# A tenth column block of the expert keys on TensorE, and eight expert blocks with a raw float32 high part

## Chip, core and metric

One core of one Trainium2 chip runs the whole program. The metric is device time in microseconds (us), the median of three runs of the kernel: 2496.15 before, from 2490.72 to 2497.42. Engines are named as in the profile: PE is the matrix engine (PEld its weight loads), DVE the vector engine, ACT the scalar engine, POOL the general one, SP issues DMA.

## What is computed

One step of a hybrid decoder layer: an input projection, an RWKV-7 group and a sparse-attention group, an output projection, a layer norm, and a PEER mixer (128 x 128 experts, of which each token picks 16 in each of 8 heads), followed by a second layer norm. There are 256 prompt tokens and 32 sample tokens, with 2048 columns. Only the mixer matters here:

```python
def block(args):
    xb, eb, gb = args
    h = jax.nn.gelu(jnp.einsum('cd,chkd->chk', xb, u_tab[eb]), approximate=False)
    return jnp.einsum('chk,chkd->cd', gb * h, v_tab[eb])
```

`u_tab` and `v_tab` have 16384 rows of 2048 float32, `eb` holds the 128 chosen experts of each token, and `gb` their gates.

## The kernel before, in words

The program is written in Python against a tile framework. A scheduler simulates the engines and puts the instructions of each engine in an order; each engine then runs its own queue strictly in that order. `tc.high_priority` lets a group go ahead, `tc.issue_after(x)` holds a group back until instruction x is placed.

The product of a token with its 128 chosen rows of `u_tab` is split by columns. UG of the 2048 columns (896 before) are done on DVE: POOL issues a gather of one chosen row per token (`fetch`, 128 tokens at a time, tile `rows`, five buffers), and one DVE instruction multiplies it with the tokens and sums it up (`dot`, line 1803). There are 256 such gathers and dots, 128 for each of two tiles of 128 prompt tokens. The other NDB blocks of 128 columns (9 before) are done on PE for all 16384 experts and all 256 prompt tokens, in 128 blocks of 128 experts (`dense`, lines 1873 to 1888): SP loads the transposed rows of the block (`ur`, three buffers), PE accumulates in one of five banks `ph`, ACT copies the result to the table AW. Six of the column blocks are split columns: ACT rounds the rows to float32r as high part `uh` (line 1639), DVE forms the low part `ul` (line 1640), in two halves of three column blocks each, and PE does three float32r matmuls for each column block, with XHd and XLd the high and low part of the tokens (line 1886). The rest of the column blocks (three before, tile Xfd) are multiplied as raw float32, straight from `ur` (line 1879).

The stages around it: the query stage ("wq") has PE do the queries and DVE choose the experts, head by head (lines 1364 to 1421, with POOL helping), and DVE do the sample tokens' dots (`sr`, line 1559). At its end come the exponential of the gates (`ge`, ACT, line 1428) and the Gelu of the sample tokens (`shT`, ACT, line 1565), which the scheduler mixes with the first blocks of the dense stage. AW lies where buffers of the query stage were, so that its first copy waits for them. Low and high parts of the first NPRI = 12 blocks have a high priority. In the dense stage one or two dots are issued behind each block's low parts: ND = 1, and one more in NDN of 8 blocks (4 before). What is left of the 256 is done in the weighing ("weigh"), spread over the first 28 of its 68 steps: a step makes one-hot tiles on DVE (`oo`, line 1918), transposes and multiplies them on PE, and DVE picks out the sums (`xj`, line 1941); in every other step DVE adds up eight sums (line 1944), ACT takes their Gelu (line 1945), and DVE multiplies with the result (line 1949) after the next `oo`. The last stage (V) multiplies the weights with `v_tab`.

Of the kernel before, what the change touches and what calls it, by code (L numbers as in the profile page):

```python
# [2 lines left out]

# [1 line left out]

# [5 lines left out]
F32 = mybir.dt.float32  # L11
F32R = mybir.dt.float32r
# [6 lines left out]
P = 128  # L19
# [3 lines left out]
NPR = 256  # L23
# [26 lines left out]
NDW = 1  # L50
NPRI = 12
ND = 1
NDN = 4
NUR = 3
NRW = 5
NDB = 9
SPLIT = ((0, 3), (3, 6))
NSP = SPLIT[-1][1]
UG = 128 * (16 - NDB)
# [93 lines left out]
def hybrid_decode_step(ctx: ExitStack, tc: tile.TileContext, a, outs, dbg=None):  # L153
    nc = tc.nc
    ve, sc, pe, gp, sy = nc.vector, nc.scalar, nc.tensor, nc.gpsimd, nc.sync
    stop = dbg.get("stop", 99) if dbg is not None else 99
# [1622 lines left out]
    dp, kc, kq = (Pool(nm, "left") for nm in ("dp", "kc", "kq"))  # L1779
    dp([P, NDB, P], "ur", bufs=NUR)  # L1780
    XHd, XLd = dp([P, NSP, NPR], "XHd", F32R), dp([P, NSP, NPR], "XLd", F32R)
# [42 lines left out]
    for h in range(9):  # L1824
        S = []
        for c in (2 * h, 2 * h + 1):
            if c < 16:
                pb = bank("pj")
                for o in range(0, 16, 8):
                    w = wq_.pop((c, o), None) or query_load(c, o)  # L1830
# [42 lines left out]
    def dense(i1):  # L1873

        w = dp([P, NDB, P], "ur", bufs=NUR)
        sy.dma_start(w.rearrange("p k e -> p (k e)"), a["peer_u_t"][P * i1:P * i1 + P, :])
        ph = bank("ph")
        for e in range(NSP, NDB):
            pe.matmul(ph[:, :NPR], w[:, e, :], Xfd[:, e - NSP, :], start=(e == NSP), stop=False)  # L1879
        for e0, e1 in SPLIT:  # L1880
            wh, wl = (dp([P, e1 - e0, P], nm, F32R, bufs=3) for nm in ("uh", "ul"))
            with tc.high_priority(offset=120 + 45 * i1 if i1 < NPRI else 0):
                lo_ = columns(w[:, e0:e1, :], wh, wl)
            for e in range(e0, e1):
                for wi, xi in ((wh, XHd), (wh, XLd), (wl, XHd)):
                    mm = pe.matmul(ph[:, :NPR], wi[:, e - e0, :], xi[:, e, :],  # L1886
                                   start=False, stop=(e == NSP - 1 and wi is wl))
        return lo_, mm, sc.copy(AW[:, i1 // 64, :, i1 % 64], ph[:, :NPR])  # L1888

    tabled = []  # L1890
    for i1 in range(P):
        lo_, mm, end = dense(i1)
        n_ = ND + (i1 * NDN % 8 < NDN)
        with tc.issue_after(lo_.ins):
            dot(min(max(P - got[1], 0) or n_, n_))
        if got[1] >= P + 8 and not tabled:
            with tc.issue_after(mm.ins), tc.issue_after(end.ins):
                table(0)
            tabled.append(0)
# [168 lines left out]
    for k in range(P):  # L2068
# [9 lines left out]
        lo_ = ve.tensor_tensor(vl, v_, vh.bitcast(F32), OP.subtract)  # L2078
# [92 lines left out]
```

## Time and profile before

| what | us |
|---|---|
| median of the runs | 2496.15 |
| the profiled execution, its own time | 2498.71 |
| its span, first to last instruction | 2496.9 |
| dense stage in the span | 1190.0 to 1682.3 |
| weighing, steps with dots | 1682.3 to 1818.2 |
| DVE busy in the span, line 1803 (the dots) | 272.0 |
| PE busy in the span, lines 1879 and 1886 (the dense stage) | 867.0 |

A busy time is a sum over the instructions of a group; what matters is whether the engine is the last to be ready in the stage where it works. PE's matmuls overlap each other in the table (a float32r matmul of 256 columns is shown with some 283 ns and follows the one before after 120), so that distances between starts are read instead. A row of the timeline has the start, the length, the engine, the line and the operation, out<-in with the tile names, and in brackets the idle time before it and what ended that.

### The profile page before, as it was taken

How to read it: one execution, taken by the hardware profiler on the slowest of the kernel's cores; microseconds unless marked ns; L12 is line 12 of the kernel's file. 1: busy time of each engine (PE TensorE's matmuls, PEld its weight loads, DVE VectorE, ACT ScalarE, POOL GpSimd, SP SyncE). 2: the span in 40 equal slices, each digit the busy share in tenths (PEclk: the TensorE clock that was granted, in tenths of full speed). 3: DMA queues.
4: the chain of work that ended last, by engine and by line, in shares of the span. 5: the costliest groups of instructions: out<-in, count | busy, mean ns of one | idle time of the engine just before them, and what ended most of it. 6: DMA issues, size and time to landing. Idle time of an engine off the chain costs nothing.

```text
span 2496.9 us, 44823 instructions
## 1 busy us (share of the span) xinstructions
PE 2246.1 (90%) x16396; PEld 1888.6 (76%) x16396; DVE 1851.9 (74%) x4241; ACT 927.4 (37%) x1848; POOL 1373.4 (55%) x1422
## 2 busy tenths in 40 slices
PE   7979999988889997789699999996699799999996
PEld 7967898875545665678598889986676688888785
DVE  5789756554563446889977776779976799988888
ACT  4433222213441333220233343434566444443433
POOL 5677423242444005478655555556656488876662
PEclk9999999998896896899899999997899899999998
DMA  7777975457668884797499999996678599999995
GB/s 219 234 235 232 272 220 172 122 178 223 214 206 269 283 299 148 282 325 241 144 385 372 370 361 357 353 336 221 216 249 294 221 369 356 362 365 361 350 358 186
DMA packets 327613, 684.23 MB, mean 274 GB/s; under 512 B 82270, under 2 KB 200992, under 8 KB 326464
## 3 DMA queue, kind: packets, MB, share of 16 engines
q1 hardware_dynamic: 246176, 342.58, 41.4%
q0 software_dynamic: 81216, 338.78, 38.4%
q8 instruction: 129, 2.11, 0.3%
q14 instruction: 92, 0.75, 0.1%
HBM read 665.69 MB, written 23.88 MB: 276 GB/s over the span
## 4 chain that ended last, share of the span: by engine, by line
PE 60%; DVE 17%; DMA 8%; issue 7%; ACT 4%; POOL 3%; SPq 1%; DVEq 0%; POOLq 0%; ACTq 0%
PE pb L2085 17%; PE ph L1886 10%; PE pj L426 8%; PE ph L1879 3%; PE pa L1668 3%; PE p L1083 2%; DVE rows L1803 2%; DMA co<-in_cache_cmp_kv,gidx 2%; DVE sr L1559 2%; PE pa L1963 2%; DVE ul L1640 2%; PE ss L1500 1%; PE px L1930 1%; PE fs L1982 1%; DVE oo L1918 1%
## 5 line engine op out<-in xcount | busy, mean ns | idle before, releaser
L457 POOL DMA_INDIRECT rows<-in_peer_u_g,gi x256 | 332.3, 1298 | 239.5 <-DVE rows L1803 195.2
L457 POOL DMA_INDIRECT rq<-in_peer_v_g,gi x256 | 378.6, 1479 | 141.8 <-DVE fP L2058 80.2
L1803 DVE SCALAR_TENSOR_TENSOR rows<-rows,x1a 128x896 f32<-128x896 f32 x256 | 272.0, 1092 | 2.9 <-DMA rows<-in_peer_u_g,gi 2.7
L1886 PE MATMUL ph<-XHd,ul 128*128 128x256 f32 x768 | 225.3, 294 | 27.6 <-DVE ul L1640 22.7
L426 PE MATMUL pj<-XH,wl 128*128 128x288 f32 (+1 forms) x752 | 230.1, 306 | 15.2 <-DVE wl L421 9.1
L426 PE MATMUL pj<-XH,wh 128*128 128x288 f32 (+1 forms) x752 | 228.2, 304 | 13.6 <-DVE ss L756 6.9
L1886 PE MATMUL ph<-XHd,uh 128*128 128x256 f32 x768 | 236.7, 308 | 0.0
L2058 DVE SCALAR_TENSOR_TENSOR fP<-rq,ge,fP 128x640 f32<-128x640 f32 x254 | 223.8, 881 | 5.9 <-DMA rq<-in_peer_v_g,gi 3.4
L426 PE MATMUL pj<-XL,wh 128*128 128x288 f32 (+1 forms) x752 | 224.5, 299 | 0.0
L1640 DVE TENSOR_TENSOR ul<-ur,uh 128x384 fp32r<-128x384 f32 x256 | 131.8, 553 | 120.1 <-ACT uh L1639 93.3
L1886 PE MATMUL ph<-XLd,uh 128*128 128x256 f32 x768 | 217.4, 283 | 0.0
L2085 PE MATMUL pb<-vl,ah 128*128 128x512 f32 (+1 forms) x768 | 207.8, 378 | 1.4 <-issue 0.5
L2085 PE MATMUL pb<-vh,ah 128*128 128x512 f32 (+1 forms) x768 | 188.0, 380 | 20.9 <-ACT vh L2077 20.9
L2085 PE MATMUL pb<-vh,al 128*128 128x512 f32 (+1 forms) x768 | 205.7, 376 | 0.0
L419 ACT CAST wh<-wraw 128x512 fp32r<-128x512 f32 (+1 forms) x188 | 114.7, 617 | 223.7 <-PE pj L426 169.0
L1879 PE MATMUL ph<-Xfd,ur 128*128 128x256 f32 x768 | 187.6, 380 | 1.1 <-DMA ur<-in_peer_u_t 1.1
L1886 PEld LDWEIGHTS ph<-XHd,ul 128*128 128x128 f32 x768 | 147.0, 192 | 42.1 <-DVE ul L1640 41.8
L2085 PEld LDWEIGHTS pb<-vh,ah 128*128 128x128 f32 x768 | 145.5, 196 | 43.8 <-ACT vh L2077 24.5
L480 DVE SCALAR_TENSOR_TENSOR CA<-co,wbc,CA 128x256 f32<-128x256 f32 x248 | 133.9, 577 | 45.5 <-DMA co<-in_cache_cmp_kv,gidx 45.2
L2085 PEld LDWEIGHTS pb<-vl,ah 128*128 128x128 f32 x768 | 145.2, 195 | 24.5 <-DVE vl L2078 4.5
L426 PEld LDWEIGHTS pj<-XH,wl 128*128 128x128 f32 (+1 forms) x752 | 142.6, 190 | 26.6 <-DVE wl L421 12.7
L1888 ACT COPY AW<-ph 128x256 f32<-128x256 f32 x128 | 77.8, 608 | 228.1 <-PE ph L1886 198.7
(854 smaller groups left out, 5472.6 us busy)
## 6 DMA issues: line engine op xcount, KB each, us to landing
ur<-in_peer_u_t SPq DMA_DIRECT2D x128, 576.0 KB
wraw<-in_w_in SPq DMA_DIRECT2D x152, 256.0 KB
cw<-in_w_out SPq DMA_DIRECT2D x32, 512.0 KB
wraw<-in_w_out SPq DMA_DIRECT2D x32, 512.0 KB
wraw<-in_peer_wq SPq DMA_DIRECT2D x32, 512.0 KB
cw<-in_peer_wq SPq DMA_DIRECT2D x32, 512.0 KB
wraw<-in_w_in SPq DMA_DIRECT2D x64, 128.0 KB
co<-in_state_win_kv SPq DMA_DIRECT2D x16, 512.0 KB
```

The costliest lines, as they stand in the source:

```text
L419: sc.copy(wh[:, :, :n], w[:, :, :n])
L426: last[2] = pe.matmul(pb[:n, :nt], wi[:, k, :n], xi[(o + k) // 8][:, (o + k) % 8, :nt], start=(o + k == 0 and wi is wh and xi is xh), stop ...
L457: gp.indirect_dma_start(out=dst, out_offset=None, in_=rows_, in_offset=bass.IndirectOffsetOnAxis(ap=ix, axis=0))
L480: ve.scalar_tensor_tensor(d_, x_, w_, d_, op0=OP.mult, op1=OP.add)
L1640: return ve.tensor_tensor(xl, pb, xh.bitcast(F32), OP.subtract)
L1668: pe.matmul(acc[t], xi[:, e, P * t:P * t + P], wi[:, e, :], start=(k == e == n_ == 0), stop=(k == 6 and e == 1 and n_ == 2))
L1803: i_ = ve.scalar_tensor_tensor(r_, r_, 1.0, X1a[t], op0=OP.mult, op1=OP.mult, accum_out=h_)
L1879: pe.matmul(ph[:, :NPR], w[:, e, :], Xfd[:, e - NSP, :], start=(e == NSP), stop=False)
L1886: mm = pe.matmul(ph[:, :NPR], wi[:, e - e0, :], xi[:, e, :], start=False, stop=(e == NSP - 1 and wi is wl))
L1888: return lo_, mm, sc.copy(AW[:, i1 // 64, :, i1 % 64], ph[:, :NPR])
L2058: ve.scalar_tensor_tensor(fP[t], r_, w_, fP[t], op0=OP.mult, op1=OP.add)
L2085: pe.matmul(acc[3 * t + q][:, :n_], wi[:, P * t:P * t + P], xi[:, 512 * q:512 * q + n_], start=(k == 0 and wi is ah and xi is vh), stop=(k ...
```

## The change

Ten column blocks go to PE and 768 columns stay with DVE (UG follows from NDB); the tenth is a raw one, four in place of three. NDN is 6, so that three in four dense blocks have two dots: 224 dots in the stage in place of 192, and 30 in place of 62 in the weighing (two are done before). In the first eight dense blocks (NFB) the six split columns are multiplied raw, `ur` with XHd, and only the product with XLd is a float32r one, with `uh`; no `ul` is formed, `uh` has no raised priority, and the dots of these blocks are not held back by their low parts. `uh` has two buffers in place of three. Lines after the edits are 1 to 10 higher.

```diff
-NDN = 4
+NDN = 6
...
-NDB = 9
+NDB = 10
+NFB = 8
...
         ph = bank("ph")
         for e in range(NSP, NDB):
             pe.matmul(ph[:, :NPR], w[:, e, :], Xfd[:, e - NSP, :], start=(e == NSP), stop=False)
+        if i1 < NFB:
+            for e in range(NSP):
+                pe.matmul(ph[:, :NPR], w[:, e, :], XHd[:, e, :].bitcast(F32), start=False, stop=False)
         for e0, e1 in SPLIT:
-            wh, wl = (dp([P, e1 - e0, P], nm, F32R, bufs=3) for nm in ("uh", "ul"))
+            if i1 < NFB:
+                wh = dp([P, e1 - e0, P], "uh", F32R, bufs=2)
+                lo_ = sc.copy(wh, w[:, e0:e1, :])
+                for e in range(e0, e1):
+                    mm = pe.matmul(ph[:, :NPR], wh[:, e - e0, :], XLd[:, e, :], start=False, stop=(e == NSP - 1))
+                continue
+            wh, wl = (dp([P, e1 - e0, P], nm, F32R, bufs=n_) for nm, n_ in (("uh", 2), ("ul", 3)))
...
-        with tc.issue_after(lo_.ins):
+        with tc.issue_after(lo_.ins) if i1 >= NFB else nullcontext():
             dot(min(max(P - got[1], 0) or n_, n_))
```

ACT's queue at the start of the dense stage, before; each `ur` number is one dense block, from block 1's second half on, and each `ph` number a block's bank:

```order
L1639 CAST uh_13421<-ur_13402 128x384
L1639 CAST uh_13444<-ur_13438 128x384
L1888 COPY AW_13356<-ph_13359 128x256
L1639 CAST uh_13457<-ur_13438 128x384
L1639 CAST uh_13483<-ur_13477 128x384
L1888 COPY AW_13356<-ph_13404 128x256
L1639 CAST uh_13496<-ur_13477 128x384
L1639 CAST uh_13519<-ur_13513 128x384
L1888 COPY AW_13356<-ph_13440 128x256
L1639 CAST uh_13532<-ur_13513 128x384
L1428 ACTIVATE ge0_73<-ge0_73 128x128
```

The same place after, where `ur_13393` is block 1, `ur_13420` block 2, `ur_13450` block 3 and `ur_13480` block 4:

```order
L1887 CAST uh_13406<-ur_13393 128x384
L1898 COPY AW_13356<-ph_13359 128x256
L1887 CAST uh_13411<-ur_13393 128x384
L1887 CAST uh_13433<-ur_13420 128x384
L1898 COPY AW_13356<-ph_13395 128x256
L1887 CAST uh_13438<-ur_13420 128x384
L1429 ACTIVATE ge0_73<-ge0_73 128x128
L1429 ACTIVATE ge1_74<-ge1_74 128x128
L1887 CAST uh_13463<-ur_13450 128x384
L1898 COPY AW_13356<-ph_13422 128x256
L1887 CAST uh_13468<-ur_13450 128x384
L1566 ACT_TABLE_LOAD
```

Block 1's second high part has moved behind the first AW copy, block 3's behind the gates' exponentials, and block 4's, with the Gelu of `shT` after the last row, behind that. Before, all of these stood ahead.

ACT in the middle of the dense stage, before, from the AW copy of one block on, and after:

```order
L1888 COPY AW_13356<-ph_15579 128x256
L1639 CAST uh_15619<-ur_15613 128x384
L1639 CAST uh_15632<-ur_15613 128x384
L1639 CAST uh_15658<-ur_15652 128x384
L1639 CAST uh_15671<-ur_15652 128x384
L1888 COPY AW_13356<-ph_15615 128x256
L1888 COPY AW_13356<-ph_15654 128x256
L1639 CAST uh_15694<-ur_15688 128x384
```

```order
L1898 COPY AW_13356<-ph_15600 128x256
L1640 CAST uh_15685<-ur_15678 128x384
L1640 CAST uh_15698<-ur_15678 128x384
L1898 COPY AW_13356<-ph_15640 128x256
L1640 CAST uh_15722<-ur_15715 128x384
L1640 CAST uh_15735<-ur_15715 128x384
L1898 COPY AW_13356<-ph_15680 128x256
```

Before, every second or third block's high parts stood behind the AW copy of the block just ahead of it (`ur_15688` behind `ph_15654`); after, both high parts of a block stand ahead of that copy throughout (`ur_15715` ahead of `ph_15680`).

DVE where the first low parts meet the dots, before, with the Gelu's input (`shT`):

```order
L1803 SCALAR_TENSOR_TENSOR rows,hd_12150<-rows,x1a 128x896
L1640 TENSOR_TENSOR ul<-ur,uh 128x384
L1564 TENSOR_TENSOR shT<-shT 128x32
L1430 RECIPROCAL sm_13341<-sm_13341 128x8
L1640 TENSOR_TENSOR ul<-ur,uh 128x384 x2
```

And after, where the input of the Gelu stands nine rows ahead of the first of these:

```order
L1804 SCALAR_TENSOR_TENSOR rows,hd_12150<-rows,x1a 128x768
L1432 TENSOR_TENSOR ge_74<-ge_74,sm_13347 128x128
L1815 TENSOR_SCALAR ii<-gi_70 128x128
L1804 SCALAR_TENSOR_TENSOR rows,hd_12150<-rows,x1a 128x768
L1816 CAST ii<-ii 128x128
L1804 SCALAR_TENSOR_TENSOR rows,hd_12150<-rows,x1a 128x768 x12
L1641 TENSOR_TENSOR ul<-ur,uh 128x384 x2
L1804 SCALAR_TENSOR_TENSOR rows,hd_12150<-rows,x1a 128x768 x2
```

Before, low parts ran between the last selections and the dots; after, 14 dots stand between the Gelu's input and the first low part, which is block 8's.

More of the change, by code (lines that the diff above doesn't have):

```diff
@@ L1 @@
 import math
-from contextlib import ExitStack
+from contextlib import ExitStack, nullcontext
 import numpy as np
```

## Prediction

> **What bounds the kernel now.** First the busy time by stage, in stretches cut where the trace changes character. The columns are the stretch, its length, busy us of PE, PEld, DVE, ACT and POOL (instructions in brackets), granted PE clock, DMA share and GB/s.
>
> ```profile
> core 0: us, PE busy (x) PEld busy (x) DVE busy (x) ACT busy (x) POOL busy (x), PEclk, DMA share, GB/s
> 1109.00:1190.00 81.00, 79.22 (x389) 70.06 (x388) 81.00 (x315) 7.80 (x22) 64.42 (x93) 1.00 0.80 243
> 1190.00:1221.40 31.40, 9.29 (x58) 8.14 (x56) 31.40 (x143) 2.48 (x6) 18.25 (x39) 0.71 0.22 72
> 1221.40:1226.50 5.10, 5.10 (x24) 5.04 (x24) 5.10 (x28) 1.54 (x4) 2.33 (x7) 0.50 0.86 285
> 1226.50:1682.30 455.80, 449.13 (x3000) 410.75 (x2999) 332.54 (x678) 179.92 (x378) 261.29 (x211) 1.00 0.96 356
> 1682.30:1818.20 135.90, 92.06 (x540) 84.62 (x539) 130.67 (x408) 62.34 (x168) 83.85 (x63) 0.77 0.70 219
> 1818.20:1967.00 148.80, 135.70 (x1026) 99.62 (x1025) 97.36 (x395) 94.34 (x250) 71.13 (x63) 0.96 0.69 230
> ```
>
> The dense stage is the third to fifth line with the second: it runs from 1190.0 to 1682.3. From 1226.5 on PE has no rest and the full clock. The sixth line is the first 28 steps of the weighing, which carry the dot products left over: there DVE is full and PE waits at a clock of 0.77. From 1190 to 1221.4 it is DVE too: PE has work for 9 us only. In the query stage (first line) both are full: the dense stage cannot start before 1190.0, and what is taken from DVE there brings all its later work forward. The change buys time of DVE and pays in time of PE, so it costs in one stretch and gains in another, and the sum is a difference of the two.
>
> Next the price of a block on PE, from its timeline. Each matmul is shown as longer than the distance to the next, so distances count.
>
> ```profile
> 1450.25 1.46 PE L1879 MATMUL ph<-Xfd,ur 128*128 128x256 f32 x6
> 1451.36 0.47 PE L1886 MATMUL ph<-XHd,uh 128*128 128x256 f32 x1
> 1451.66 0.28 PE L1886 MATMUL ph<-XLd,uh 128*128 128x256 f32 x1
> ...
> 1453.70 1.46 PE L1879 MATMUL ph<-Xfd,ur 128*128 128x256 f32 x6
> ...
> 1455.11 0.28 PE L1886 MATMUL ph<-XLd,uh 128*128 128x256 f32 x1
> 1455.46 0.38 PE L1886 MATMUL ph<-XHd,ul 128*128 128x256 f32 x1
> ...
> 1457.47 0.81 PE L1879 MATMUL ph<-Xfd,ur 128*128 128x256 f32 x3
> ```
>
> A block takes three raw float32 matmuls (six passes) and 18 float32r ones. From 1451.66 to 1453.70 there are 17 float32r matmuls: 0.120 us each. The block takes 3.45 us from 1450.25, so the six raw passes are left with 3.45 - 2.16 = 1.29, 0.215 each. The query stage says the same of raw passes alone:
>
> ```profile
> 1181.93 7.07 PE L1832 MATMUL pj<-XT,wraw 128*128 128x256 f32 x32
> 1188.84 1.34 PE L1378 MATMUL pb<-SKT,QP 128*128 128x128 f32 x8
> ```
>
> 32 passes in 6.91 us, 0.216 each: a raw matmul costs 0.432, a float32r one 0.120. The next block in the timeline takes 3.77, because PE stands from 1455.11 to 1455.46 for the low part. Over the long stretch 124 blocks take 455.8 us, 3.68 each, so 0.23 a block is this wait.
>
> Last, the start of the dense stage, on PE, ACT and DVE:
>
> ```profile
> 1190.01 1.46 PE L1879 MATMUL ph<-Xfd,ur 128*128 128x256 f32 x6
> 1221.40 0.58 PE L1886 MATMUL ph<-XHd,ul 128*128 128x256 f32 x1 [21.74 <-DVE ul L1640]
> ```
> ```profile
> 1205.70 0.59 ACT L1888 COPY AW<-ph 128x256 f32<-128x256 f32 x1 [10.90 <-issue]
> 1229.58 0.51 ACT L1428 ACTIVATE ge<-ge 128x128 f32<-128x128 f32 x2
> 1237.60 0.23 ACT L1565 ACTIVATE shT<-shT 128x32 f32<-128x32 f32 x1 [1.61 <-DVE shT L1564]
> ```
> ```profile
> 1117.72 0.54 DVE L1640 TENSOR_TENSOR ul<-ur,uh 128x384 fp32r<-128x384 f32 x1
> 1204.25 1.22 DVE L1559 SCALAR_TENSOR_TENSOR sr<-sr,sx 128x1024 f32<-128x1024 f32 x1
> 1220.80 0.55 DVE L1640 TENSOR_TENSOR ul<-ur,uh 128x384 fp32r<-128x384 f32 x1
> 1221.27 1.08 DVE L1803 SCALAR_TENSOR_TENSOR rows<-rows,x1a 128x896 f32<-128x896 f32 x1
> 1222.28 0.55 DVE L1640 TENSOR_TENSOR ul<-ur,uh 128x384 fp32r<-128x384 f32 x1
> 1236.91 0.55 DVE L1640 TENSOR_TENSOR ul<-ur,uh 128x384 fp32r<-128x384 f32 x1
> 1237.39 0.18 DVE L1564 TENSOR_TENSOR shT<-shT 128x32 f32<-128x32 f32 x1
> ```
>
> PE's gap of 21.7 us waits for a low part that DVE has no time for. The three rows of ACT are not about blocks: the first AW copy follows the last sample dot (DVE, 1204.25), the gates' exponential and the Gelu follow DVE's last selection of experts. All three stand in ACT's queue among the high parts.
>
> **The dense stage from the ninth block.** Each of the 120 blocks gets one raw matmul more: 2.16 + 4 x 0.432 = 3.89 us. Does the wait of 0.23 stay? In the changed order of ACT both high parts of the next block stand ahead of the AW copy, and the second can start as soon as the block ends. It then needs 0.51 (ACT) and 0.47 (DVE), and PE first asks for it after 1.73 + 1.08 + 0.24 = 3.05 us. DVE has 0.94 of low parts and 1.75 dots in a block. A dot costs 1.01 (1221.27 to 1222.28), and with 768 instead of 896 columns 0.88 by my estimate (0.87 in proportion, and some of it is fixed). That is 2.5 of 3.89 us. So I take 0.01 a block; bounds 0 and 0.1 (12 us).
>
> The DMA moves more: 590 to 655 KB of transposed rows a block, while the gathered rows stay at 688 KB (1.5 x 459, now 1.75 x 393). That is 1.28 MB in 3.68 us before (348 GB/s of the 356 shown) and 1.34 MB in 3.90 after, 345: no more than it gives now, but at a share of 0.96 there is no reserve, and part of the 0.1 is for that.
>
> In one place the Trainium skill would price this otherwise. FP8 and Floating Point Precision, TensorE Precision Notes, says that true FP32 takes four passes through the array. If a pass is the 0.120 of a float32r matmul, an estimate by that page is 0.48 a raw matmul and 4.08 a block, 23 us more in the stage. The trace has 0.432 in two stages, so the sum goes by that.
>
> **The first eight blocks.** Each takes ten raw matmuls and six float32r ones, 4.32 + 0.72 = 5.04 us, against 3.45: dearer on PE by 1.6, free of DVE. Low parts of these blocks were on DVE three times before 1190 and eight times from 1205 to 1237 (first and last of each are in the rows), 0.47 each, so the last sample dot ends 1.4 us sooner, the gates 4.4 sooner with the shorter dot, and the Gelu 5.4 sooner. ACT is still served in order. Block 0: 1190.0 to 1195.0. Block 1 does its raw matmuls by 1199.4, and its second high part stands behind the AW copy (1204.3) and is ready at 1205.4: end 1205.8. Block 2: 1210.9. Block 3 has its raw part by 1215.2, then waits for a high part behind the gates: 1225.2 + 0.51 + 0.51, one AW copy, the other half: end 1227.8. Block 4's raw part ends at 1232.1, its high part waits for the Gelu (1232.3): end 1234.5. Blocks 5 to 7: 1249.6. Bounds of 3 us either way.
>
> Block 8 needs its first low part 1.73 + 0.24 after that, at 1251.6. On DVE, 14 dots stand ahead of it behind the Gelu's input (rows of the order above), and these wait for gathers:
>
> ```profile
> 1237.19 1.16 POOL L457 DMA_INDIRECT rows<-in_peer_u_g,gi  x1
> ```
> ```profile
> 1242.06 1.09 DVE L1803 SCALAR_TENSOR_TENSOR rows<-rows,x1a 128x896 f32<-128x896 f32 x1
> 1244.71 1.09 DVE L1803 SCALAR_TENSOR_TENSOR rows<-rows,x1a 128x896 f32<-128x896 f32 x1 [0.41 <-DMA rows<-in_peer_u_g,gi]
> 1250.91 1.09 DVE L1803 SCALAR_TENSOR_TENSOR rows<-rows,x1a 128x896 f32<-128x896 f32 x1 [0.49 <-DMA rows<-in_peer_u_g,gi]
> ```
>
> The third gather is issued at 1237.19, behind DVE's selection, so now at 1232.4. From there DMA must bring 14 x 393 KB and four loads of 655 KB, 8.1 MB: 22.8 us at 356 GB/s. The last dot is done at about 1257 and the low part at 1257.5, so PE stands for 6 us. The bounds are 0 (DVE work alone: 14 x 0.88 and 3 us of small ones end by 1247.4) and 13 (dots 2.07 us apart, as from 1244.71 to 1250.91). After it PE is cold: in the stretch 1221.4 to 1226.5 above, 24 matmuls took 0.21 us each at a clock of 0.50. That is 2 us more. The Trainium skill (TensorE: Matmul & The Clock Gate, What's actually happening) has the half clock after one idle window of about 3.4 us; the trace agrees, 0.50 here.
>
> The dense stage ends at 1249.6 + 8 + 120 x 3.90 = 1725.6, which is 43 us later.
>
> **The weighing.** 62 dots were left for it, 30 now are (28 steps, one each, two steps with two).
>
> ```profile
> L1803 DVE SCALAR_TENSOR_TENSOR rows<-rows,x1a 128x896 f32<-128x896 f32 x62 | 65.0, 1086 | 1.1 <-DMA rows<-in_peer_u_g,gi 1.1
> L1918 DVE TENSOR_TENSOR oo<-CT,TB 128x1024 f32<-128x1024 f32 x30 | 36.6, 1220 | 0.0
> L1941 DVE SCALAR_TENSOR_TENSOR xj<-px,oo 128x128 f32<-128x128 f32 x112 | 32.4, 289 | 2.9
> ```
> ```profile
> 1749.17 1.22 DVE L1918 TENSOR_TENSOR oo<-CT,TB 128x1024 f32<-128x1024 f32 x1
> ...
> 1751.63 0.17 DVE L1944 TENSOR_TENSOR E<-E,TB 128x8 f32<-128x8 f32 x1
> 1751.72 1.08 DVE L1803 SCALAR_TENSOR_TENSOR rows<-rows,x1a 128x896 f32<-128x896 f32 x1
> ...
> 1753.76 0.20 ACT L1945 ACTIVATE E<-E 128x8 f32<-128x8 f32 x1
> ...
> 1754.75 1.22 DVE L1918 TENSOR_TENSOR oo<-CT,TB 128x1024 f32<-128x1024 f32 x1
> ```
>
> A step without dots is 2.55 us of DVE (1749.17 to 1751.72), 28 of them 71.4; with 62 x 1.01 that is 134, nearly the whole stretch. With 30 x 0.88 it is 97.8. What is late next is the Gelu: it ends at 1753.96, 2.24 after the sum that it reads, and DVE multiplies with its result behind the next one-hot tile. With two dots and that tile (1.14) DVE comes to it after 3.2; with one dot after 2.0, so it waits 0.3 in every other step, and where PE's clock is down, and with it what stands ahead of the Gelu on ACT, up to three times that by my estimate. 14 such waits are 4 to 13 us; I take 8. The stretch takes 106 instead of 136: 30 us gained, bounds 22 and 37. Later steps have no dots and stay.
>
> **Sum.** +43 - 30 = +13 us. The profiled execution took 2498.71 us, 1.8 more than its span, so it would take 2511.7. It lies 2.6 over the median of the runs, 2496.15, and the change of that median is the forecast: 2509 us.
>
> **Rivals.**
> *Break even.* The stall at block 8 does not come, since DMA moves more than 356 GB/s while PE asks for little, and the Gelu is in time: 1249.6 + 466.5 = 1716.1, +34, against -37. That is 2493. For it: DMA was nearly idle before 1221. Against it: the dots waited for gathers around 1250 even before.
> *Faster.* ACT does not hold the first eight blocks up: they run through in 40.3 us, to 1230.3, and 120 x 3.89 later it is 1697, +15, against -30: 2481. It decides at block 3: its last pass would have to be over by 1216. For it: PE is free and the loads are early. Against it: the order has the exponential ahead of that block's high part, and DVE reaches its input only at 1225.
> *Much slower.* DMA, at a share of 0.96, becomes the bound, or the loop of high part, low part and copy costs 0.2 a block again: 24 us more, 2533. A weighing held by PE at half clock adds up to 8 to either.
> *Not as described.* The raw blocks could be built otherwise than told; the order shows ten raw matmuls and six of float32r in each of eight blocks, so this has no chance of its own.
> *A dearer raw matmul.* Four passes of 0.120 are 0.48, and 120 x 4 x 0.048 brings it to 2532. For it: the raw ones now follow each other in longer rows. Against it: so they do in the query stage, at 0.432.
>
> **How the numbers follow.** The forecast has 0.51, breaking even 0.27, faster 0.08, much slower 0.12, the dearer raw matmul 0.02. The likeliest case's own range is 2500 to 2523. The range reaches into break even and much slower: 2491 to 2527. About 0.3% (7.5 us) is what a measurement of this kernel can tell from no change. Faster by over that is the faster rival and the edge of break even, 0.10; within it nearly all of break even and the lower edge of the forecast, 0.28; slower 0.62.
>
> **What would show it.** Right: blocks from the tenth on 3.88 to 3.92 us apart on PE; ten raw matmuls in a row in eight blocks at 5.04; PE idle behind ACT in blocks 1 and 3, and behind DVE at block 8; the first AW copy near 1204, the Gelu near 1232; weighing steps of 3.4 to 3.8 us up to the 28th. Wrong: a dense stage that ends before 1716 or after 1740; a block of 4 us or more with PE waiting for the transposed rows (DMA is the bound); weighing steps still above 4 us (the DVE was not what held them); or a difference outside the dense stage and the 28 steps, since nothing else is touched.

## The result, and the profile after

The changed kernel takes 2508.2 us, the median of 12 runs, against 2492.8 for 12 runs of the kernel before on the same chip; the ratio is 1.007, with a 95% interval from 1.0049 to 1.0091. It is slower by about as much as forecast. The profiled execution took 2509.64 us with a span of 2507.9.

The busy time by stage of the changed kernel, in stretches like those shown of before and with the same columns (stretch, length, busy us of PE, PEld, DVE, ACT and POOL, granted PE clock, DMA share, GB/s):

```profile
1188.00:1246.80 58.80, 46.34 (x210) 40.17 (x209) 51.03 (x206) 12.10 (x28) 41.25 (x69) 0.85 0.46 159
1246.80:1261.50 14.70, 5.73 (x28) 5.32 (x28) 10.00 (x21) 1.89 (x4) 10.15 (x9) 0.70 0.88 303
1261.50:1724.80 463.30, 463.30 (x3101) 437.57 (x3099) 308.93 (x654) 182.58 (x357) 214.86 (x206) 1.00 0.95 342
1724.80:1829.00 104.20, 71.94 (x541) 65.12 (x541) 97.37 (x345) 62.46 (x168) 54.44 (x34) 0.95 0.48 143
1829.00:1977.00 148.00, 135.38 (x1025) 98.47 (x1024) 97.72 (x398) 94.27 (x250) 71.52 (x63) 0.96 0.69 230
```

The dense stage (first three lines) runs from 1188.0 to 1724.8: 536.8 us against 492.4, so 44.4 more. From 1261.5 on PE has not a moment's rest. The 28 weighing steps with dots (fourth line) take 104.2 us against 135.9, at a PE clock of 0.95 where it was 0.77. The steps behind them (148.0 against 148.8) are as before. The dense stage began 2.0 us earlier in this execution, with nothing changed ahead of it: in all the profiled executions of this study its start lies between 1176.5 and 1209.4, so durations of stages are compared below, not spans.

The pace of a block, from PE's timeline in the middle of the stage:

```profile
1502.81 1.89 PE L1880 MATMUL ph<-Xfd,ur 128*128 128x256 f32 x8
1506.69 1.89 PE L1880 MATMUL ph<-Xfd,ur 128*128 128x256 f32 x8
```

From block 10 on, 113 of the 117 distances are 3.88 us. Before, they were 3.45 and some 3.78 by turns, 3.65 in the mean from block 9 on (the prediction's mean of 3.68 has waits ahead of block 9 in it).

The first nine blocks, on PE (rows with a wait, and the beginning of blocks 1, 8 and 9), ACT and DVE:

```profile
1193.05 1.89 PE L1880 MATMUL ph<-Xfd,ur 128*128 128x256 f32 x8
1202.88 1.01 PE L1889 MATMUL ph<-XLd,uh 128*128 128x256 f32 x3 [5.00 <-ACT uh L1887]
1222.99 1.83 PE L1889 MATMUL ph<-XLd,uh 128*128 128x256 f32 x6 [7.47 <-ACT uh L1887]
1246.85 1.89 PE L1880 MATMUL ph<-Xfd,ur 128*128 128x256 f32 x8
1257.94 0.58 PE L1896 MATMUL ph<-XHd,ul 128*128 128x256 f32 x1 [8.97 <-DVE ul L1641]
1261.53 2.62 PE L1880 MATMUL ph<-Xfd,ur 128*128 128x256 f32 x8
```
```profile
1201.92 0.59 ACT L1898 COPY AW<-ph 128x256 f32<-128x256 f32 x1 [8.52 <-DVE HV L1367]
1221.84 0.69 ACT L1429 ACTIVATE ge<-ge 128x128 f32<-128x128 f32 x2 [16.99 <-DVE ge L1428]
1228.84 0.23 ACT L1566 ACTIVATE shT<-shT 128x32 f32<-128x32 f32 x1 [3.78 <-DVE shT L1565]
```
```profile
1232.87 0.96 DVE L1804 SCALAR_TENSOR_TENSOR rows<-rows,x1a 128x768 f32<-128x768 f32 x1 [1.01 <-DMA rows<-in_peer_u_g,gi]
1236.21 0.96 DVE L1804 SCALAR_TENSOR_TENSOR rows<-rows,x1a 128x768 f32<-128x768 f32 x1 [2.03 <-DMA rows<-in_peer_u_g,gi]
1256.45 0.96 DVE L1804 SCALAR_TENSOR_TENSOR rows<-rows,x1a 128x768 f32<-128x768 f32 x1
1257.34 1.02 DVE L1641 TENSOR_TENSOR ul<-ur,uh 128x384 fp32r<-128x384 f32 x2
```

PE waits 5.0 us for block 1's second high part, behind the AW copy at 1201.92; 7.5 us for block 3's, behind the exponential at 1221.84; and 9.0 us in block 8 for the first low part, which DVE forms at 1257.34 behind dots whose rows arrive from 1232.87 on. Block 9 begins 73.5 us after the start of the stage; before it did so after 58.6 (1248.62). So 14.9 of the 44.4 us are lost in the first nine blocks, and 29.5 by the pace of the other 119.

DVE in the 28 steps, by groups, and two steps of its timeline:

```profile
L1804 DVE SCALAR_TENSOR_TENSOR rows<-rows,x1a 128x768 f32<-128x768 f32 x32 | 30.3, 952 | 0.8 <-DMA rows<-in_peer_u_g,gi 0.8
L1959 DVE TENSOR_TENSOR TB<-E,TB 128x8 f32<-128x8 f32 x13 | 2.2, 166 | 1.9 <-ACT E L1955 1.9
```
```profile
1756.23 1.22 DVE L1928 TENSOR_TENSOR oo<-CT,TB 128x1024 f32<-128x1024 f32 x1
1759.66 1.22 DVE L1928 TENSOR_TENSOR oo<-CT,TB 128x1024 f32<-128x1024 f32 x1
1761.05 0.17 DVE L1959 TENSOR_TENSOR TB<-E,TB 128x8 f32<-128x8 f32 x1 [0.17 <-ACT E L1955]
1763.22 1.22 DVE L1928 TENSOR_TENSOR oo<-CT,TB 128x1024 f32<-128x1024 f32 x1
```

32 dots of 0.95 us stand where 62 of 1.09 stood. The steps take 3.43 and 3.56 us in turn, and the Gelu is late by 0.17 in every other step, 1.9 us in all.

### The profile page after: what moved, and what is told of

The parts are those of the page before. It is cut to its first block, busy times and chain, and to the rows that moved or that the text cites. A ratio compares the mean times of both kernels' runs of the same rounds, so it can differ in the third digit from the quotient of the medians.

```text
span 2507.9 us, 45265 instructions
## 1 busy us (share of the span) xinstructions
PE 2274.0 (91%) x16652; PEld 1927.3 (77%) x16652; DVE 1827.5 (73%) x4225; ACT 939.1 (37%) x1848; POOL 1335.5 (53%) x1422
## 4 chain that ended last, share of the span: by engine, by line
PE 65%; DVE 14%; DMA 9%; issue 5%; POOL 4%; ACT 2%; SPq 1%; DVEq 0%; POOLq 0%; ACTq 0%
PE pb L2095 18%; PE ph L1896 10%; PE ph L1880 8%; PE pj L427 8%; PE pa L1669 2%; PE p L1084 2%; DVE sr L1560 2%; PE pa L1973 2%; DMA co<-in_cache_cmp_kv,gidx 2%; PE px L1940 1%; PE fs L1992 1%; PE ss L1501 1%; PE pt L1932 1%; DMA big<-in_state_rwkv 1%; PE sa L925 1%
## 5 line engine op out<-in xcount | busy, mean ns | idle before, releaser
L458 POOL DMA_INDIRECT rows<-in_peer_u_g,gi x256 | 286.7, 1120 | 297.5 <-DVE rows L1804 270.5
L1804 DVE SCALAR_TENSOR_TENSOR rows<-rows,x1a 128x768 f32<-128x768 f32 x256 | 243.3, 961 | 12.4 <-DMA rows<-in_peer_u_g,gi 12.3
L1880 PE MATMUL ph<-Xfd,ur 128*128 128x256 f32 x1024 | 246.4, 384 | 0.0
L1640 ACT CAST uh<-ur 128x384 fp32r<-128x384 f32 x240 | 122.7, 513 | 291.0 <-PE ph L1896 281.3
L1896 PE MATMUL ph<-XHd,uh 128*128 128x256 f32 x720 | 226.4, 314 | 0.0
L1896 PE MATMUL ph<-XHd,ul 128*128 128x256 f32 x720 | 204.4, 284 | 9.0 <-DVE ul L1641 9.0
L1880 PEld LDWEIGHTS ph<-Xfd,ur 128*128 128x128 f32 x1024 | 188.0, 193 | 21.6 <-DMA ur<-in_peer_u_t 0.2
L1896 PE MATMUL ph<-XLd,uh 128*128 128x256 f32 x720 | 203.9, 283 | 0.0
## 6 DMA issues: line engine op xcount, KB each, us to landing
wraw<-in_w_in SPq DMA_DIRECT2D x152, 256.0 KB
```

The costliest lines, as they stand in the source:

```text
L458: gp.indirect_dma_start(out=dst, out_offset=None, in_=rows_, in_offset=bass.IndirectOffsetOnAxis(ap=ix, axis=0))
L1640: sc.copy(xh, pb)
L1804: i_ = ve.scalar_tensor_tensor(r_, r_, 1.0, X1a[t], op0=OP.mult, op1=OP.mult, accum_out=h_)
L1896: mm = pe.matmul(ph[:, :NPR], wi[:, e - e0, :], xi[:, e, :], start=False, stop=(e == NSP - 1 and wi is wl))
```

## The experiments

Twelve kernels were run. For each, the profiled execution gives two durations: the dense stage, from the first raw matmul of block 0 to the end of the last matmul into `ph`, and the weighing, from there to the start of its last one-hot tile (`oo`). Behind that the executions differ by less than 3 us. The last column is the number of dots that begin behind the dense stage. The ratio is that of the runs, with its 95% interval, to the kernel before on the same chip.

| kernel | ratio | dense | weighing | sum, against before | dots behind |
|---|---|---|---|---|---|
| before | 1 | 492.4 | 257.9 | 0 | 62 |
| changed | 1.0070 (1.0049 to 1.0091) | 536.8 | 224.9 | +11.4 | 32 |
| no raw blocks | 1.0069 (1.0041 to 1.0098) | 530.3 | 237.3 | +17.3 | 38 |
| raw blocks alone | 1.0034 (1.0014 to 1.0054) | 500.4 | 255.2 | +5.3 | 62 |
| dots alone | 1.0006 (0.9987 to 1.0025) | 501.0 | 259.6 | +10.3 | 51 |
| early dots later | 1.0096 (1.0066 to 1.0127) | 527.7 | 240.6 | +18.0 | 43 |
| both parts raw | 1.0102 (1.0072 to 1.0131) | 548.1 | 222.5 | +20.3 | 30 |
| dots stay | 1.0496 (1.0464 to 1.0528) | 622.0 | 248.2 | +119.9 | 62 |
| eight split | 1.0087 (1.0054 to 1.0120) | 546.0 | 225.1 | +20.8 | 30 |
| fewer dots | 1.0083 (1.0055 to 1.0110) | 476.9 | 294.6 | +21.2 | 94 |
| one more operation in weighing | 1.0129 (1.0097 to 1.0161) | 536.6 | 246.5 | +32.8 | 32 |
| four raw blocks | 1.0064 (1.0038 to 1.0089) | 529.3 | 231.3 | +10.3 | 36 |
| dots stay, in order | 1.0146 (1.0113 to 1.0179) | 534.4 | 246.8 | +30.9 | 62 |
| before, in order | 1.0043 (1.0023 to 1.0063) | 496.2 | 256.0 | +1.9 | 62 |

One execution's sum can lie 9 us off what its ratio says (dots alone, before in order), so a difference of a few us in that column decides nothing by itself.

### The parts of the change

**No raw blocks.** From the changed kernel:

```diff
-NFB = 8
+NFB = 0
```

> The changed kernel with the constant for raw blocks at 0: ten column blocks, six dots in eight blocks more than one, but low parts from the first block on. Theory (the raw form costs time: its eight blocks of 5.03 us, their holds behind ScalarE's queue and the wait of 9 us in block 8): the profile of before begins its block 13 at 1263.11 us where the changed kernel begins its block 9 at 1261.53 and was 2.0 us earlier at block 0, so some four blocks of 3.68 us, 15 us, are lost by the raw form; here the first low part should come at about 1219 to 1221 as before, the dense stage should end near 1711, weighing stay at 104 us, and the time be 2490 to 2497, 12 to 18 us under the changed kernel and level with before (0.997 to 1.002). Rival (the raw form saves the wait of 21.7 us that before shows for its first low part): 2515 to 2530, slower than the changed kernel.

The time is that of the changed kernel. Theory and rival both fall. PE's waits:

```profile
1220.40 0.58 PE L1896 MATMUL ph<-XHd,ul 128*128 128x256 f32 x1 [19.50 <-DVE ul L1641]
1227.18 3.58 PE L1880 MATMUL ph<-Xfd,ur 128*128 128x256 f32 x8 [3.20 <-DMA ur<-in_peer_u_t]
```

The wait for the first low part is back (19.5 us), and behind it come waits for columns. Block 9 begins at 1259.08, 67.6 us after the start, so the raw form costs some 6 us there, not 15: with ten column blocks the first nine are slow without it too. The dense stage gains 6.5 us, but six more dots stand behind it and weighing is 12.4 us longer; its dots wait 4.4 us for rows there, against 0.8 in the changed kernel.

**Raw blocks alone.** From the changed kernel:

```diff
-NDN = 6
+NDN = 4
...
-NDB = 10
+NDB = 9
```

> The kernel before (nine column blocks, one dot and four in eight more) with its first eight blocks in the raw form. Block: 3 x 0.432 + 6 x 0.432 + 6 x 0.120 = 4.61 us. Theory (the raw form costs 15 us): block 1 held until 1203, block 3 until 1223 or so, block 8's first low part behind the twelve dots at about 1255, then block 13 near 1278 where before has 1263; weighing as before: 2505 to 2511, ratio 1.005 to 1.008. Rival (the raw form frees TensorE of the wait for low parts): 2470 to 2485. Second rival (only a stage bound by DMA moved: what is lost ahead is made up behind): 2490 to 2498.

The dense stage is 8.0 us longer and the number of dots behind it the same; the ratio says 8. The sign is the theory's, the size half. The wait of block 8 is there with nine column blocks too:

```profile
1248.74 0.58 PE L1896 MATMUL ph<-XHd,ul 128*128 128x256 f32 x1 [6.09 <-DVE ul L1641]
```

**Dots alone.** From the kernel before:

```diff
-NDN = 4
+NDN = 6
```

> The kernel before with six dots in eight blocks beside one a block instead of four: 32 dots of 458 KB each move from weighing to the dense stage, nothing else. Theory (the DMA has no reserve): 590 KB of columns and 1.75 x 458 KB of rows a block are 1.39 MB; at 348 to 356 GB/s 3.91 to 4.0 us a block instead of 3.68, +27 to +38 us, against -30 us in weighing: 2488 to 2502, level with before. Rival (the DMA can give the 372 GB/s that the profile of before shows from 1262 to 1400): 3.74 us a block, +7 us, so 2465 to 2475, faster than before by some 1 per cent, and the tenth column block was not needed to make room.

Level with before, as the theory had it, but by another way. Of the 32 dots only 11 left the stretch behind the dense stage: the scheduler's order has 21 in one heap ahead of weighing's first product. The windows of the dense stage from block 9 on, and DVE's group in the heap:

```profile
1235.20:1400.00 164.80, 162.03 (x1073) 146.99 (x1072) 121.51 (x239) 62.76 (x135) 90.27 (x74) 1.00 0.98 373
1400.00:1677.60 277.60, 271.37 (x1792) 246.13 (x1790) 202.63 (x404) 104.80 (x224) 151.39 (x125) 0.99 0.97 362
```
```profile
L1803 DVE SCALAR_TENSOR_TENSOR rows<-rows,x1a 128x896 f32<-128x896 f32 x21 | 22.8, 1093 | 8.6 <-DMA rows<-in_peer_u_g,gi 8.5
```

The DMA is busy to 0.98 and 0.97, and the 11 dots more cost the dense stage 8.6 us. In the heap the dots wait 8.6 us for rows. That the DMA had no room for the others isn't shown: from block 9 on PE waits only 2.9 us for columns, and the heap is the scheduler's doing.

**Dots stay.** From the changed kernel:

```diff
-NDN = 6
+NDN = 4
```

> The changed kernel with four instead of six dots in eight blocks: the tenth column block and the raw form stay, but 28 to 30 dots go back to weighing. Theory (the 31 us that weighing lost are the dots that moved, and the dense stage is bound by TensorE at 3.88 us a block whatever the dots): the dense stage takes 532 to 537 us, its DMA share falls from 0.95 to some 0.87, weighing takes 250 us or so from the dense stage's end to its last product of indices instead of 225: time 2525 to 2536, ratio to before 1.014 to 1.020. Rival (dots cost the dense stage what they save behind it): the dense stage shrinks to 510 us and the time stays at 2505 to 2512.

Neither: 5% slower. PE's group of raw matmuls from block 10 to the dense stage's end, and two rows of its timeline in the middle:

```profile
L1880 PE MATMUL ph<-Xfd,ur 128*128 128x256 f32 x944 | 234.3, 391 | 64.5 <-DMA ur<-in_peer_u_t 64.2
```
```profile
1508.03 1.99 PE L1880 MATMUL ph<-Xfd,ur 128*128 128x256 f32 x8 [1.24 <-DMA ur<-in_peer_u_t]
1509.67 0.47 PE L1896 MATMUL ph<-XHd,ul 128*128 128x256 f32 x1
```

PE waits 64.5 us for columns, though the DMA has less to move. The last row shows why it may hurt: the pass with a low part (`ul`) at 1509.67 is one of a block two ahead of the one whose raw matmuls, waiting for their load, stand before it. A block has eight raw instructions and 18 other passes, so the trace can be counted through: in 117 of the 127 transitions, all from block 11 on, a block's raw matmuls begin before the passes of the blocks ahead are done. From block 15 on 25 or 27 passes are still to come, that is the whole block ahead and part of the one before it. In the changed kernel there is no such transition. Raw matmuls that are late then hold up the blocks ahead, with them the copies into their buffers, and so the next load. The Trainium skill (PSUM — Partial Sum Buffer, Engine vs sequencer instructions) says that matmuls start and complete in program order; the trace agrees, since the pass at 1509.67 runs only behind the raw matmuls that waited until 1508.03.

**Dots stay, in order.** The run before, with the raw matmuls held behind the last pass of the block ahead:

```diff
-        for e in range(NSP, NDB):
-            pe.matmul(ph[:, :NPR], w[:, e, :], Xfd[:, e - NSP, :], start=(e == NSP), stop=False)
+        with tc.issue_after(last_mm[-1].ins) if last_mm else nullcontext():
+            for e in range(NSP, NDB):
+                pe.matmul(ph[:, :NPR], w[:, e, :], Xfd[:, e - NSP, :], start=(e == NSP), stop=False)
...
         lo_, mm, end = dense(i1)
+        last_mm.append(mm)
```

> The run in which the dots stay, with one constraint more: a block's raw matmuls come in TensorE's order behind the last pass of the block ahead. In that run 56 of the 120 later blocks had them ahead of the last low-part pass, and TensorE waited 51.8 us for columns between 1260 and 1700; in the changed kernel none of the 119 later ones. Theory (that order, not the dots, made its dense stage 571 us): here blocks come 3.88 us apart, the dense stage takes 530 to 537 us, and weighing, with 30 dots more than the changed kernel at 0.7 us (the doubled operation) to 1.15 us (the run with fewer dots) each, 246 to 260 us instead of 225: time ratio to before 1.014 to 1.021. Rival (the dots' place on VectorE, or the load behind it, made it): the dense stage stays over 555 us and the time over 1.03 of before.

As the theory had it: the dense stage is back at 534.4, so the constraint on the order was worth 88 us, and PE has no wait for columns left (463.50 of 463.50 us busy below). The expectation's count of 56 blocks is too low; it is the 117 above. Now the question of the run before is answered too. Windows of the dense stage from block 9 on and of the steps behind it, and the dots' group there:

```profile
1262.00:1725.50 463.50, 463.50 (x3101) 437.94 (x3100) 291.23 (x599) 183.13 (x358) 199.02 (x179) 1.00 0.92 319
1725.50:1850.00 124.50, 77.96 (x538) 71.01 (x538) 120.63 (x402) 62.39 (x167) 76.72 (x62) 0.90 0.69 203
```
```profile
L1804 DVE SCALAR_TENSOR_TENSOR rows<-rows,x1a 128x768 f32<-128x768 f32 x62 | 56.6, 953 | 0.0
```

With 30 dots fewer in it the dense stage is 2.4 us shorter, so PE sets its pace whatever the dots. Weighing takes 21.9 us more than in the changed kernel, 0.73 a dot. The rest of what weighing lost, 257.9 - 246.8 = 11.1 us, is there with 62 dots as well: the same dots on narrower rows. By the distance between dots, 1.01 before and 0.88 now, 62 of them make 8 of it; the other 3 us were not traced.

### The prices one by one

**One more operation in weighing.** From the changed kernel; the operation writes a tile that has no reader left, and the outcome stays:

```diff
             dot(-(-left * (s_ + 1) // 28) + 2 * P - left - got[1], keep=True)
+            pin(ve.scalar_tensor_tensor(X1a[0], X1a[0], 0.0, X1a[0], op0=OP.mult, op1=OP.mult,
+                                        accum_out=x4p([P, 1], "sp", bufs=2)))
```

> The changed kernel with one more operation of VectorE in each of weighing's first 28 steps, of a dot's size (128 x 768, two operands, summed) on a tile that nobody reads any more and without a gather. Theory (VectorE sets the pace of these steps, so that 28 to 32 dots taken out of them are worth what they last): 28 x 0.88 to 0.96 us is 25 to 27 us, the last dot comes 125 to 130 us after the dense stage's end instead of 102, and the time is 2529 to 2541, 1.015 to 1.020 of before. Rival (the steps wait for Gelu, TensorE or rows, and VectorE has room): 0 to 8 us more, 2506 to 2516.

28 operations bring 21.6 us, 0.77 each, where they last 0.95:

```profile
L2019 DVE SCALAR_TENSOR_TENSOR x1a<-x1a 128x768 f32<-128x768 f32 x28 | 26.7, 953 | 0.0
```

The stretch is DVE's, as the theory says; some of its waits are filled by the new operation, so the size is 4 us under the forecast. The ratio's middle, 1.0129, is under the forecast's edge of 1.015, and its interval reaches into it.

**Fewer dots.** From the kernel before:

```diff
-NDN = 4
+NDN = 2
```

> The kernel before with two instead of four dots in eight blocks: 33 dots of 458 KB go from the dense stage to weighing. Theory (the 0.2 us a block that before loses over its 3.45 us are the DMA's, at a share of 0.97 to 0.99): blocks come 3.45 to 3.50 us apart, the dense stage takes 470 to 477 us instead of 492, weighing 30 to 36 us more: 2498 to 2507, ratio 1.004 to 1.008. Rival (the 0.2 us are the wait for the low part behind ScalarE's copy): blocks stay at 3.65, dense at 490, and the time is 2515 to 2525, ratio 1.012 or more.

The dense stage falls to 476.9 us, and weighing grows by 36.7 for 32 dots, 1.15 each. In the middle blocks follow by 3.45 us:

```profile
1505.78 1.46 PE L1879 MATMUL ph<-Xfd,ur 128*128 128x256 f32 x6
1509.23 1.46 PE L1879 MATMUL ph<-Xfd,ur 128*128 128x256 f32 x6
```

The wait of 0.23 a block is gone there, and the ratio is at the upper edge of the theory's. But the cause is not the theory's. The scheduler's order on ACT changed with the dots, from two blocks' high parts and then two AW copies to one and one, and the trace of before tells the two causes apart. The block of before that begins at 1453.70 and takes 3.77 us, on ACT and DVE:

```profile
1453.90 0.60 ACT L1888 COPY AW<-ph 128x256 f32<-128x256 f32 x1 [2.83 <-PE ph L1886]
1454.30 0.92 ACT L1639 CAST uh<-ur 128x384 fp32r<-128x384 f32 x2
1454.84 1.03 DVE L1640 TENSOR_TENSOR ul<-ur,uh 128x384 fp32r<-128x384 f32 x2 [1.83 <-ACT uh L1639]
```

Its high parts stand behind the AW copy of the block just ahead, which waits for that block's last pass; DVE is idle for 1.83 us until the first of them comes, and PE then waits for the low part. In blocks 14 to 126 of before, 68 stand so, two in three and later every second. Of these 67 take 3.77 us or more, while 44 of the 45 others, whose high parts stand ahead of that copy, take 3.44 or 3.45. The two kinds alternate in one stretch at the same mean DMA share, 0.98 and 0.97, and PE waits nowhere there for columns. So the wait is that of ACT's order, as the prediction had it, at 0.33 in a part of the blocks. Whether the DMA would have carried 3.45 us for every block with as many dots isn't shown; here, with fewer, its share is a little down:

```profile
1249.20:1663.50 414.30, 411.65 (x2840) 388.79 (x2839) 284.71 (x551) 179.90 (x353) 182.41 (x155) 1.00 0.94 341
```

**Eight split.** From the changed kernel:

```diff
-NFB = 8
+NFB = 0
...
-SPLIT = ((0, 3), (3, 6))
+SPLIT = ((0, 2), (2, 4), (4, 6), (6, 8))
...
-(("uh", 2), ("ul", 3))
+(("uh", 3), ("ul", 3))
```

> Ten column blocks, no raw form, eight of the ten instead of six in three float32r passes (four pairs of column blocks a block of experts, high and low parts in three buffers of two): 8 x 3 x 0.120 + 2 x 0.432 = 3.74 us a block instead of 3.89. Theory (TensorE sets the dense stage's pace, the DMA only just follows): blocks 3.75 us apart, 16 us less than the run without raw blocks, 2488 to 2497, level with before. Rival (at a share of 0.95 the DMA has no room): 0.95 x 3.88 / 3.74 is 0.985, blocks stay at 3.83 to 3.88 and the time at 2502 to 2510. Second rival (ScalarE's and VectorE's smaller pieces come too late): slower, 2510 to 2525.

The second rival. PE's blocks in the middle:

```profile
1507.32 1.03 PE L1880 MATMUL ph<-Xfd,ur 128*128 128x256 f32 x4
1511.59 1.03 PE L1880 MATMUL ph<-Xfd,ur 128*128 128x256 f32 x4
1515.33 1.03 PE L1880 MATMUL ph<-Xfd,ur 128*128 128x256 f32 x4
```

The second of these takes 3.74 us, as the prices say; the one before it 4.27, since its first high and low parts come late. That is ACT's order again: of blocks 14 to 126, 48 have their high parts behind the AW copy of the block just ahead, and 47 of them take over 4.2 us, while 56 of the 65 others take 3.73 or 3.74. So the matmul prices hold. That the pieces are smaller is not shown to be the trouble; an order without such blocks was not tried.

### The first blocks

**Both parts raw.** From the changed kernel:

```diff
-NFB = 8
+NFB = 5
...
                 pe.matmul(ph[:, :NPR], w[:, e, :], XHd[:, e, :].bitcast(F32), start=False, stop=False)
+                mm = pe.matmul(ph[:, :NPR], w[:, e, :], XLd[:, e, :].bitcast(F32), start=False, stop=(e == NSP - 1))
+            lo_ = mm
...
-                wh = dp([P, e1 - e0, P], "uh", F32R, bufs=2)
-                lo_ = sc.copy(wh, w[:, e0:e1, :])
-                for e in range(e0, e1):
-                    mm = pe.matmul(ph[:, :NPR], wh[:, e - e0, :], XLd[:, e, :], start=False, stop=(e == NSP - 1))
                 continue
```

> The changed kernel with five instead of eight raw blocks, and in them both parts of X against the raw columns: 4 + 6 + 6 raw matmuls, 16 x 0.432 = 6.91 us a block, and no copy by ScalarE at all. Theory (ScalarE's copies, queued behind the copy of the outcome and behind the gates' exponential, hold the first blocks): the five blocks run through in 34.6 us from the dense stage's start with no wait over 1 us, where the changed kernel took 43.7 us for five; block 5's and 6's low parts then wait behind the dots, whose rows land from 45 us on, so block 9 begins 62 to 69 us after the start instead of 73.5, and the time is 2495 to 2503. Rival (what comes first decides nothing, since the gathers' transfers set when the low parts come): block 9 begins at 72 to 75 us as before, and the time is 2504 to 2512.

The five blocks do run through, from 1195.94 to 1230.48, 34.5 us without a wait. Then it all comes:

```profile
1237.91 0.58 PE L1894 MATMUL ph<-XHd,uh 128*128 128x256 f32 x1 [5.54 <-ACT uh L1640]
1246.87 0.58 PE L1894 MATMUL ph<-XHd,ul 128*128 128x256 f32 x1 [8.16 <-DVE ul L1641]
1258.87 0.58 PE L1894 MATMUL ph<-XHd,ul 128*128 128x256 f32 x1 [5.21 <-DVE ul L1641]
```

PE waits 5.5 us for a high part behind the Gelu and 8.2 and 5.2 for low parts behind dots. What was gained ahead is lost: block 9 begins 72.3 us after the start, as the rival had it. ACT's holds are real, but not what ends the early part. The time is worse than the rival's, 1.0102. In this build 88 transitions have a block's raw matmuls ahead of passes of the blocks before, as in the run where the dots stay, and from block 9 on PE waits 6.7 us for columns; that this makes the difference was not tried by itself.

**Four raw blocks.** From the changed kernel:

```diff
-NFB = 8
+NFB = 4
```

> The changed kernel with four raw blocks instead of eight. Theory (what ends the early part is VectorE's work on the gates and then the rows of the first dots, which land from 44 us after the dense stage's start on; how many blocks are raw moves only where TensorE waits): the four end after 36.6 us as in the changed kernel, block 4 waits for its low part until about 52, block 9 begins at 69 to 74 us (73.5 in the changed kernel, 68.6 without raw blocks), and the time is 2502 to 2512, 1.005 to 1.009 of before. Rival (each raw block costs its 1.15 us and ScalarE's holds): 5 to 10 us less, 2496 to 2503.

```profile
1243.28 1.83 PE L1889 MATMUL ph<-XLd,uh 128*128 128x256 f32 x6 [8.76 <-ACT uh L1887]
1256.76 0.58 PE L1896 MATMUL ph<-XHd,ul 128*128 128x256 f32 x1 [6.44 <-DVE ul L1641]
```

The hold behind the exponential (8.8 us) and the wait for the first low part (6.4 us) are there as in the changed kernel. Block 9 begins after 66.0 us (1275.44), a little under the theory's range, and the dense stage is 7.5 us shorter; four more dots behind it give 6.4 back. Eight, four or no raw blocks: the time is the same.

**Early dots later.** From the changed kernel:

```diff
-NDN = 6
+NDN = 7
...
+        if i1 < NFB:
+            continue
         n_ = ND + (i1 * NDN % 8 < NDN)
-        with tc.issue_after(lo_.ins) if i1 >= NFB else nullcontext():
+        with tc.issue_after(lo_.ins):
```

> The changed kernel without dots in its first eight blocks; seven instead of six in eight blocks beside one a block from block 8 on, so that the fourteen dots follow later. Theory (the first low part of block 8 waits for VectorE, which waits for the gathers of the fourteen dots ahead of it): the wait of 9.0 us and the 2 us of half clock behind it go, block 9 begins 10 to 12 us earlier (near 1250), blocks stay at 3.88 us (1.39 MB a block, 359 GB/s), and some eleven of the dots that come after the last low part add up to 10 us ahead of weighing: 2496 to 2508. Rival (the low part waits for something else, ScalarE's copies or the columns' load): block 9 stays at 1261, time 2508 to 2520.

The wait of 9 us is gone; DVE now waits for the high part instead of rows (first row), and the dense stage is 9.1 us shorter, as expected. But eleven dots more are behind it, in a heap that waits for rows (second row, DVE's group in the first 28 us), and weighing is 15.7 us longer. The time is outside the theory's range. In this build, too, raw matmuls stand ahead of passes of the blocks before, from block 9 to block 27, and PE waits 4.2 us for columns there, so the dots' place is not the only thing that changed.

```profile
1240.57 1.03 DVE L1641 TENSOR_TENSOR ul<-ur,uh 128x384 fp32r<-128x384 f32 x2 [13.56 <-ACT uh L1640]
```
```profile
L1804 DVE SCALAR_TENSOR_TENSOR rows<-rows,x1a 128x768 f32<-128x768 f32 x17 | 16.2, 958 | 5.8 <-DMA rows<-in_peer_u_g,gi 5.6
```

**Before, in order.** The constraint of the run above, in the kernel before.

> The kernel before with the same constraint. In its order 3 of 127 blocks, all among the first twelve, have their raw matmuls ahead of the last low-part pass of the block ahead. Theory (its steady blocks are bound by DMA, so that TensorE's order matters in the first twelve alone): within 0.3 per cent of before, 0.997 to 1.002. Rival (those raw passes fill TensorE's wait of 21.7 us for its first low part): 4 to 8 us slower, 1.002 to 1.004.

The rival, at its upper edge: 0.43% slower. In before, blocks 2 to 8 have their raw matmuls ahead (seven, not the three of the expectation). Without that PE's wait for the first low part is longer, since the raw matmuls of the next blocks no longer fill it:

```profile
1224.93 0.58 PE L1887 MATMUL ph<-XHd,ul 128*128 128x256 f32 x1 [24.49 <-DVE ul L1640]
```

## Why the prediction was right, point by point

**The pace.** The step had 3.89 us of matmuls and 0.01 of wait; it is 3.88, with no wait. The dearer raw matmul falls with it, and in the run with eight split columns the price came out again, at 3.74 of 3.74 in the blocks without a wait. The much slower rival falls too: PE is busy for 463.3 of 463.3 us.

**The wait of 0.23.** The prediction put it down to the low part behind ACT's order, and the trace of before bears that out, block by block: 3.77 us or more with the high parts behind the AW copy, 3.45 with them ahead, at the same DMA share. In the changed kernel, where 112 of the 113 blocks 14 to 126 have them ahead, the wait is gone. From block 9 on it was 0.20 in the mean; the 0.23 had the waits of earlier blocks in it.

**No reserve in the DMA.** Not decided. The arithmetic of 345 GB/s was right (342), and PE didn't wait. Dots alone brought only 11 of 32 dots into the stage of before, but PE's waits for columns there were small.

**The first eight blocks.** Holds and order were right: 1201.9 against 1204.3 for the AW copy, 1221.8 against 1225.2 for the exponential, 1228.8 against 1232.3 for the Gelu, block 7's end at 1246.9 against 1249.6; that is 2.4 to 3.5 us early all along, with a start that was 2.0 early. The stall at block 8 was mis-sized: 9.0 us, not 6. The low part came when it was forecast (1257.3 against 1257.5); PE came to it 2.8 us sooner. In this order the low part hangs on the rows, not on PE, so each us that PE gains ahead of it is stood out there. The two cold us behind it are in the trace (block 9 begins 3.6 us after PE goes on, for passes worth 1.9). All in all the first nine blocks cost 14.9 us more than before, where the prediction's times make it 12.9.

**What decides the first blocks.** Here a step of the prediction failed, if not its number: the faster rival was to be decided by ACT's holds, at block 3. With the holds of the raw blocks gone (both parts raw; one behind the Gelu was left for block 5) nothing was gained, because the low parts behind the dots' rows are next, and with fewer raw blocks the dense stage's gain of 7.5 us came back as dots in weighing. The raw form, by itself a loss of 0.34% with nine column blocks, costs nothing that can be measured with ten.

**The weighing.** 30 us were forecast, of 136; 31.7 came. Two terms were off, and they cancel in part. The Gelu's wait was too high, 8 us: it measured 1.9. The prediction allowed for up to three times 0.3 in every other step where PE's clock is down; the clock was 0.95 and the wait 0.17. Why the clock rose isn't shown. The dots were too few: 32 are behind the dense stage, not 30. With both put right the prediction's sum is 71.4 + 28.2 + 1.9 = 101.5 of the 104.2 measured. The experiments split the whole weighing's 33.0 us: 21.9 by the dots that moved (dots stay, in order) and 11.1 by what was there without moving them, most of it the narrower rows.

**The sum.** +44.4 and -33.0 leave +11.4 in the profiled executions, and the runs say 0.7%, 17 us; the forecast was +13. The profiled executions don't show where the 6 us between the two lie, so that the hit is this close is in part luck. Where did the gain of moving dots go? Moving them pays some 19 us, once the tenth column block is there (from 1.0146 to 1.0070). The tenth block, which makes the room for them, costs 31 by the profile and 36 by the runs, with its raw blocks (dots stay, in order). The tenth block buys time of DVE and DMA with time of PE, and at these prices it is dearer than what it moves. No version here beats the kernel before.

## What to carry to other kernels

When work is moved off an engine, price what makes room for it apart from what the room is used for: here the use paid 19 us and the room cost over 31. A wait that is removed ahead of a point that something else sets (here the arrival of gathered rows) is waited out at that point, so look for what would be late next before counting it. And after any edit to a scheduled program compare the order on the engine that has no rest: raw matmuls that wait for a load, queued ahead of the passes of the blocks before, cost 88 us, more than all that the edits were about. The same holds for the queue that feeds it: high parts behind a copy instead of ahead of it cost 0.33 us in each of the slower blocks of the kernel before.

## What the runs showed of the hardware

A float32r matmul of 256 columns follows another by 0.120 us, a raw float32 one by 0.432, 3.6 times as much; a raw one is two instructions of 0.216. The Trainium skill (TensorE: Matmul & The Clock Gate, Wait — 56ns, not 53.3ns?) gives a warm pass of N columns N / 2.4 GHz and 2.5 ns; an estimate by it is 0.109 us, and four of them are 0.437, next to the 0.432 of the trace. So the price of a raw matmul fits four such passes, and the float32r one is a little dearer than a pass; the prediction's estimate of 0.48 had counted four of the latter.

The DMA's share of busy time fell more slowly than what it moved: 375 GB/s at 0.99 (before, 1248.6 to 1400), 342 at 0.95 (changed), 319 at 0.92 (dots stay, in order), 267 at 0.82 (dots stay), which is 379, 360, 347 and 326 GB/s for a full share. A share of 0.95 did not mean that PE was about to wait, and one of 0.82 did not mean that it wouldn't. The rows of the second and the third stand above; the first and the fourth:

```profile
1248.60:1400.00 151.40, 149.57 (x993) 136.08 (x992) 111.13 (x221) 58.88 (x126) 85.29 (x70) 1.00 0.99 375
1262.70:1810.00 547.30, 481.93 (x3074) 441.88 (x3072) 278.27 (x595) 183.74 (x354) 200.24 (x176) 0.99 0.82 267
```
